# A fp32 diffusion block on one core: accumulators, weight rings, the cut of the feed-forward and the place of modulation units

## The chip, the core and the metric

The kernel runs on one core of one Trainium2 chip. The metric is the device time of one execution in microseconds (us). The five engines that matter here are TensorE (PE in the profile; PEld is its loading of weights), VectorE (DVE), ScalarE (ACT), GpSimd (POOL) and SyncE (SP), which issues nearly all DMAs, in the order of the program.

## What is computed

Two layers of a diffusion backbone over 512 main tokens and 256 context tokens, model width 1024. Each layer has a modulated norm, three token mixers (windowed attention, a bidirectional gated recurrence, a chunked MLP) merged by gates, an output projection, and a SwiGLU feed-forward of 2816 hidden columns. In the last layer only the main tokens are needed. The parts that the change touches are:

```python
g = sigmoid(gate)                                    # gate = h @ w_in[:, gate columns]
m = g0 * (a @ w_br[0]) + g1 * (b @ w_br[1]) + g2 * (c @ w_br[2])
x = x + g1mod * (m @ w_o)
h = rmsnorm(x, norm2_g[l]) * (1.0 + sc2) + sh2
x = x + g2mod * ((silu(h @ w_gate) * (h @ w_up)) @ w_down)
# sh1, sc1, g1, sh2, sc2, g2 = split(silu(c) @ w_ada[l] + b_ada[l], 6), and the same for the context
```

Everything is fp32.

## The kernel before

**Tiles.** Activations lie with channels on the partitions and tokens (T = 768, main and context together, in layer 1 512) along the free axis. A matrix product goes tile by tile: `dense` takes 128 output columns, loads their weights (`load_raw`, a DMA on SP's queue, L279), and computes over 8 (or 4, or 2) blocks of 128 input channels. fp32 is made of three matmuls of a short format: weights and activations are split into a high part (ACT, L288 and L349 for weights, L730 for activations) and a low part (VectorE, L289, L350, L731), and PE sums high x high, high x low and low x high (L306). A whole tile of 768 tokens needs columns of 512 and 256 in two PSUM banks, so a dense tile with 8 input blocks has 24 steps of two matmuls each.

**Weight buffers.** Pools `wraw`, `whi`, `wlo` hold 3, 2 and 2 slots of 4 KB per partition. A slot is taken for every weight tile whatever its size, and also for every block of modulation weights (`wra`, L535).

**The feed-forward of layer 0.** Its 22 hidden tiles are worked in pieces (`FF_PIECES[0]`): per piece the gate and up tiles, then the 8 down tiles of that piece, added to the residual `X` by VectorE (L778). The first `FF_PLAIN` tiles are plain `dense` tiles (L1333, L1336). All other tiles are taken in pairs by a scheme of seven products in place of eight (`seven`): the input channels, the two output tiles and the tokens are halved, and seven products of 4 input blocks x 128 columns x 384 tokens (`product`, 12 matmuls, L405) are combined. They come in the order B11, B21, N2, N1, T3, B22, T4 and use four sets of weights: g1 (B11, B21), g2 (N2, N1), g3 (T3, B22), g4 (T4 alone). g2 and g3 are split from sums of raw weights that POOL makes (`s21`, `s34`, L426). There are two sevens per pair, gate and up. Results are evacuated between the products: ACT copies partial results u1, u2 and u5 out of PSUM (L434, L440, L442), and `take` combines them on VectorE (L463, L465).

`al` and `ga`, the accumulators of B11+N2+T3+T4 and of N1+B22, are the two banks of one 1024-wide PSUM tile `pa`; `be` (B21) is a bank `pb` of its own. Waits are set by tile: an instruction that writes a tile waits until earlier readers of that tile have finished.

**Activation sums.** `seven_acts` makes the four sums N1, N2, T3 and T4 of the activations (POOL L370, VectorE L374 to L378) and splits them. It is a generator; before, its whole body for all four block pairs is issued behind the first plain tile.

**Modulation units.** The next layer's modulation vectors come from `ada_units`: a unit (512 columns of `w_ada`) is four steps; a step loads 512 KB (L536) and adds two blocks of it, scaled by one entry of silu(c), into an accumulator per token kind (`nb`) (the first block on ACT, L520, the others on VectorE, L522). The fourth step folds the accumulators (L497, L498), and the last unit of a group spreads the result (a matmul, L507). Steps wait in `ada_queue`, and `fill(n)` issues n of them at that place in the program. Layer 1's units 0 to 3 (nb 2, 16 steps) are queued behind layer 0's merge and issued at every down tile of layer 0's feed-forward. Units 4 to 7 and 8 to 11 (nb 1, 16 steps each) are queued at layer 1's merge (L1272) and issued two per merge tile (L1296).

**Order.** Each engine works its instructions in the order in which the program lists them; a scheduler puts them in that order from the code, and PE follows the code closely.

## Time and profile before

| | us |
|---|---|
| median of 3 runs | 2583.61 (2577.85 to 2583.71) |
| the profiled execution | 2584.96 |
| its span in the profile | 2583.0 |
| granted PE clock over the span | 0.987 |
| layer 0's feed-forward, first plain tile to the end | 905 to 1558 |
| layer 1's merge, about | 1960 to 2110 |

A row of waits reads: engine, what it was to write and in which line, what it waited for, then the sum of us, how often, and the longest. A row of the timeline reads: start, duration, engine, line, operation, output<-inputs, shape, and in brackets the idle time before and its releaser. A row of a group ends with count, busy us, mean ns, and idle time before.

### The profile page before, as it was taken

What the parts mean: (1) busy time and instruction counts of PE and PEld (TensorE: products, weight loads), DVE (VectorE), ACT (ScalarE), POOL (GpSimd) and SP (SyncE); (2) the same over time, 40 slices, a digit from 0 to 9 for tenths busy, and PEclk for the clock granted to TensorE, in tenths of its full rate; (3) what the DMA queues carried; (4) which work ended last, traced back from release to release, by engine and by line L of the source; (5) the groups of instructions that cost most, each with busy time, mean ns of one, the idle gap of its engine ahead of it and who ended that gap; (6) DMA issues with size and microseconds to landing.
All of it is one profiled execution on the core that took longest, in us unless ns stands there. A gap on an engine that the chain in (4) does not pass through costs nothing. (4 is left out here: it accounts for less than half of the span.)

```text
span 2583.0 us, 34315 instructions
## 1 busy us (share of the span) xinstructions
PE 2428.9 (94%) x13582; PEld 2088.2 (81%) x13582; DVE 1549.7 (60%) x2648; ACT 904.4 (35%) x1520; POOL 325.6 (13%) x231
## 2 busy tenths in 40 slices
PE   8899999999999978788989888999999899999998
PEld 4888888888888867777878777888787689888888
DVE  4688787764453576474444456767887655534335
ACT  3333354442222432323232234334544234322224
POOL 0001100000211240302112132010000112000001
PEclk9999999999999989999999999999999999999999
DMA  7222111123432313231212222111226644333234
GB/s 280 76 81 74 41 42 38 33 86 115 142 107 68 100 57 103 65 118 50 71 44 66 66 80 84 42 41 50 58 58 179 204 139 140 104 107 97 85 105 130
DMA packets 358031, 234.23 MB, mean 91 GB/s; under 512 B 8368, under 2 KB 329328, under 8 KB 357872
## 3 DMA queue, kind: packets, MB, share of 16 engines
q1 hardware_dynamic: 353936, 219.47, 28.6%
q0 software_dynamic: 2304, 10.49, 1.1%
q8 instruction: 107, 1.75, 0.3%
q10 hardware_dynamic: 1632, 2.10, 0.2%
q14 instruction: 52, 0.43, 0.1%
HBM read 224.68 MB, written 7.34 MB: 90 GB/s over the span
## 5 line engine op out<-in xcount | busy, mean ns | idle before, releaser
L288 ACT ACTIVATE wh<-wr 128x1024 fp32r<-128x1024 f32 (+4 forms) x340 | 301.7, 888 | 850.3 <-PE pd L306 604.1
L289 DVE TENSOR_TENSOR wl<-wr,wh 128x1024 fp32r<-128x1024 f32 (+4 forms) x340 | 350.7, 1033 | 209.0 <-ACT wh L288 205.7
L306 PE MATMUL pd<-hh,wh 128*128 128x512 f32 (+1 forms) x1504 | 461.8, 363 | 11.5 <-ACT gt L1282 7.2
L306 PE MATMUL pd<-hh,wl 128*128 128x512 f32 (+1 forms) x1504 | 451.1, 356 | 0.4
L306 PE MATMUL pd<-hl,wh 128*128 128x512 f32 (+1 forms) x1504 | 450.0, 355 | 0.0
L306 PEld LDWEIGHTS pd<-hh,wh 128*128 128x128 f32 x1504 | 249.0, 190 | 45.4 <-ACT gt L1282 10.1
L306 PEld LDWEIGHTS pd<-hh,wl 128*128 128x128 f32 x1504 | 249.6, 190 | 43.7 <-DVE wl L289 4.4
L306 PEld LDWEIGHTS pd<-hl,wh 128*128 128x128 f32 x1504 | 249.1, 190 | 34.2
L522 DVE SCALAR_TENSOR_TENSOR acc<-wra,sc,acc 128x512 f32<-128x512 f32 x224 | 166.3, 772 | 93.8 <-DMA wra<-in_w_ada 69.9
L306 PE MATMUL pd<-guh,wh 128*128 128x512 f32 (+1 forms) x576 | 172.8, 345 | 7.5 <-ACT wh L288 6.9
L306 PE MATMUL pd<-guh,wl 128*128 128x512 f32 (+1 forms) x576 | 171.4, 343 | 4.7 <-DVE wl L289 4.6
L306 PE MATMUL pd<-gul,wh 128*128 128x512 f32 (+1 forms) x576 | 170.7, 341 | 0.3 <-DVE gul L731 0.3
L306 PE MATMUL pd<-fl,wh 128*128 128x512 f32 (+1 forms) x432 | 160.7, 379 | 5.7 <-DVE fl L701 5.7
L306 PE MATMUL pd<-fh,wl 128*128 128x512 f32 (+1 forms) x432 | 160.2, 378 | 5.9 <-DVE wl L289 5.8
L306 PE MATMUL pd<-fh,wh 128*128 128x512 f32 (+1 forms) x432 | 159.3, 377 | 2.8 <-DVE silu L1337 2.2
L778 DVE SCALAR_TENSOR_TENSOR X<-pd,mod,X 128x256 f32<-128x256 f32 (+1 forms) x160 | 84.0, 559 | 111.5 <-PE pd L306 111.3
L306 PEld LDWEIGHTS pd<-guh,wh 128*128 128x128 f32 x576 | 98.1, 190 | 23.9 <-ACT wh L288 10.3
L306 PEld LDWEIGHTS pd<-guh,wl 128*128 128x128 f32 x576 | 98.3, 191 | 19.7 <-DVE wl L289 7.3
L306 PEld LDWEIGHTS pd<-gul,wh 128*128 128x128 f32 x576 | 98.1, 190 | 13.7 <-DVE gul L731 1.1
L405 PE MATMUL pa<-fh,wh 128*128 128x384 f32 x240 | 85.5, 356 | 24.9 <-DVE ptmp L463 7.3
L1294 POOL TENSOR_TENSOR macc<-macc,gt 128x768 f32<-128x768 f32 (+1 forms) x32 | 60.3, 1884 | 337.7 <-DVE gt L1291 331.1
L650 POOL TENSOR_TENSOR sqa<-sqa,sq 128x256 f32<-128x256 f32 (+1 forms) x40 | 50.8, 1269 | 412.5 <-ACT sq L648 412.4
(277 smaller groups left out, 4630.6 us busy)
## 6 DMA issues: line engine op xcount, KB each, us to landing
wr<-in_w_in SPq DMA_DIRECT2D x116, 512.0 KB, 3.8
wra<-in_w_ada SPq DMA_DIRECT2D x80, 512.0 KB, 3.8
wr<-in_w_ffn_gate SPq DMA_DIRECT2D x44, 512.0 KB, 3.9
wr<-in_w_ffn_up SPq DMA_DIRECT2D x44, 512.0 KB, 3.9
wr<-in_w_out SPq DMA_DIRECT2D x32, 512.0 KB, 3.7
wr<-in_w_branch SPq DMA_DIRECT2D x48, 256.0 KB, 3.1
wr<-in_w_ffn_down SPq DMA_DIRECT2D x40, 256.0 KB, 2.7
wr<-in_w_ffn_down SPq DMA_DIRECT2D x24, 384.0 KB, 3.1
```

What stands on the lines that cost most here:

```text
L288: nc.scalar.activation(out=h, in_=r, func=AF.Copy)
L289: nc.vector.tensor_tensor(out=o, in0=r, in1=h.bitcast(F32), op=ALU.subtract)
L306: nc.tensor.matmul(ps[:, b0:b1], lhsT=w[:, k, :], rhs=x[:, b0:b1], start=b not in first, stop=(k == kt - 1 and i == 2), skip_group_check=True)
L405: nc.tensor.matmul(out, lhsT=a[:, k0 + k, :], rhs=x, start=first, stop=(k == KD // 2 - 1 and i == 2), skip_group_check=True)
L522: nc.vector.scalar_tensor_tensor(out=acc[:, 0:512], in0=w, scalar=sc, in1=acc[:, 0:512], op0=ALU.mult, op1=ALU.add)
L650: eng.tensor_tensor(out=acc[:, c0:c1], in0=acc[:, c0:c1], in1=sq[:, c0:c1], op=ALU.add)
L778: self.nc.vector.scalar_tensor_tensor(out=self.X[m][:, c0:c1], in0=ps[:, c0:c1], scalar=gcol(b, m), in1=self.X[m][:, c0:c1], op0=ALU.mult, ...
L1294: nc.gpsimd.tensor_tensor(out=mm, in0=mm, in1=gt[:, 0:tt], op=ALU.add)
```

## The change

1. `ga` becomes a bank `pg` of its own, `al` the first half of a tile of its own. `ptmp` becomes one page of 768 in place of two: u5 takes the place of u1.
2. The three weight pools become rings of 12, 8 and 8 KB from which a tile takes only its own size (2 KB for 4 input blocks, 1 KB for 2).
3. `FF_PLAIN` goes from 2 to 4 and the pieces of layer 0 from (4,4,4,4,4,2) to (4,2,4,4,4,4): the first piece is four plain tiles, and 18 sevens are left of 20. `seven_acts` is issued a block pair at a time beside the second to fourth plain tile.
4. Modulation units 4 to 7 of layer 1 are queued with units 0 to 3 behind layer 0's merge. In layer 0's feed-forward a step is issued per pair of tiles by sevens and at every second down tile; in layer 1's merge one per tile, and none in the first branch.

```diff
--- before.py
+++ after.py
@@ -27,8 +27,8 @@
 HD = 64
 DK = 128
 LEVELS = 7
-FF_PIECES = ((4, 4, 4, 4, 4, 2), (5, 5, 6, 6))
-FF_PLAIN = 2
+FF_PIECES = ((4, 2, 4, 4, 4, 4), (5, 5, 6, 6))
+FF_PLAIN = 4
 H = T // 2
 NPAGES = 27
 BLOCK_US = 0.8
@@ -109,9 +109,9 @@
         self.cp = ctx.enter_context(tc.tile_pool(name="const", bufs=1))
         self.pages = Pages(ctx.enter_context(tc.tile_pool(name="pages", bufs=1)), NPAGES)
         self.dr = ctx.enter_context(tc.tile_pool(name="spill", bufs=1, space=bass.MemoryType.DRAM))
-        self.wr = ctx.enter_context(tc.tile_pool(name="wraw", bufs=3))
-        self.wh = ctx.enter_context(tc.tile_pool(name="whi", bufs=2))
-        self.wl = ctx.enter_context(tc.tile_pool(name="wlo", bufs=2))
+        self.wr = ctx.enter_context(tc.tile_pool(name="wraw", bufs=1)).ring(3 * D * 4, name="wrawr")
+        self.wh = ctx.enter_context(tc.tile_pool(name="whi", bufs=1)).ring(2 * D * 4, name="whir")
+        self.wl = ctx.enter_context(tc.tile_pool(name="wlo", bufs=1)).ring(2 * D * 4, name="wlor")
         self.sm = ctx.enter_context(tc.tile_pool(name="small", bufs=4))
         self.sp = ctx.enter_context(tc.tile_pool(name="parts", bufs=1))
         self.pd = ctx.enter_context(tc.tile_pool(name="psd", bufs=2, space=bass.MemoryType.PSUM))
@@ -275,16 +275,16 @@
 
 
     def load_raw(self, wap, kt):
-        raw = self.wr.tile([P, KD, P], F32, tag="wr", name=self.nm("wr"))
-        self.nc.sync.dma_start(out=raw[:, 0:kt, :], in_=wap.rearrange("(k p) c -> p k c", p=P))
+        raw = self.wr.tile([P, kt, P], F32, name=self.nm("wr"))
+        self.nc.sync.dma_start(out=raw, in_=wap.rearrange("(k p) c -> p k c", p=P))
         return raw
...
@@ -338,17 +338,12 @@
             self.step_chain()
 
 
-    def high_low(self, parts):
-
...
+    def high_low(self, src):
+
+        n = src.shape[1]
+        hi = self.wh.tile([P, n // P, P], F32R, name=self.nm("wh"))
+        lo = self.wl.tile([P, n // P, P], F32R, name=self.nm("wl"))
+        self.split(src, *(t.rearrange("p k c -> p (k c)") for t in (hi, lo)))
         return hi, lo
 
     def seven_acts(self, act):
@@ -359,35 +354,42 @@
...
+        held, last, whole = [], [], []
+        for k in range(KD // 2 + 1):
+            if k < KD // 2:
+                whole.append([self.single("b1"), self.single("b2")])
+                for r, (h, l) in zip(whole[k], (act[k], act[k + KD // 2])):
+                    nc.gpsimd.tensor_tensor(out=r[:, 0:T], in0=h[:, 0:T].bitcast(F32), in1=l[:, 0:T].bitcast(F32),
+                                            op=ALU.add)
+            if k > 0:
...
+            yield None
         for k, (t, t4) in enumerate(last):
             h1, l1 = act[k]
             self.split(t4, h1[:, H:T], l1[:, H:T])
@@ -424,29 +426,28 @@
         for o, x, y in ((s1, r2[:, 0:n], r2[:, n:2 * n]), (s2, s1, r1[:, 0:n]), (s3, r1[:, 0:n], r2[:, 0:n]),
                         (s4, s2, r1[:, n:2 * n])):
             nc.gpsimd.tensor_tensor(out=o, in0=x, in1=y, op=ALU.add)
-        ps = self.pd.tile([P, 1024], F32, tag="pd", name=self.nm("pa"))
-        al, ga = ps[:, 0:H], ps[:, 512:512 + H]
-        be = self.bank("pb")[:, 0:H]
-        tmp = self.pair("ptmp")
-        u1, u2, u5 = tmp[:, 0, 0:H], tmp[:, 0, H:T], tmp[:, 1, 0:H]
-        g1 = self.high_low([r1])
+        al = self.pd.tile([P, 1024], F32, tag="pd", name=self.nm("pa"))[:, 0:H]
+        be, ga = self.bank("pb")[:, 0:H], self.bank("pg")[:, 0:H]
+        tmp = self.single("ptmp")
+        u1, u2, u5 = tmp[:, 0:H], tmp[:, H:T], tmp[:, 0:H]
+        g1 = self.high_low(r1)
         self.product(al, g1, 0, q["B11"], True)
         nc.scalar.copy(out=u1, in_=al)
         self.product(be, g1, KD // 2, q["B21"], True)
         take(0, 0, be, u1)
-        g2 = self.high_low([s21])
+        g2 = self.high_low(s21)
         self.free(sa)
         self.product(al, g2, 0, q["N2"], False)
         nc.scalar.copy(out=u2, in_=al)
         self.product(ga, g2, KD // 2, q["N1"], True)
         nc.scalar.copy(out=u5, in_=ga)
-        g3 = self.high_low([s34])
+        g3 = self.high_low(s34)
         self.free(sb)
         self.product(al, g3, 0, q["T3"], False)
         take(1, 1, al, u5)
         self.product(ga, g3, KD // 2, q["B22"], False)
         take(0, 1, ga, u2)
-        g4 = self.high_low([r2[:, n:2 * n]])
+        g4 = self.high_low(r2[:, n:2 * n])
         self.product(al, g4, 0, q["T4"], False)
         take(1, 0, al, None)
         self.free(tmp)
@@ -488,6 +489,7 @@
                 self.split(s[:, t, 0:T], hp[:, t, 0:T], lp[:, t, 0:T])
                 gu.append((hp[:, t, :], lp[:, t, :]))
             self.free(s)
+            self.fill(1)
 
 
     def ada_fold(self, acc, part):
@@ -532,7 +534,7 @@
                 self.parts = self.sp.tile([P, 128], F32, tag="parts", name=self.nm("parts"))
             if q == 0:
                 state["accs"] = [self.single("acc") for _ in range(nb)]
-            raw = self.wr.tile([P, 2, 512], F32, tag="wr", name=self.nm("wra"))
+            raw = self.wr.tile([P, 2, 512], F32, name=self.nm("wra"))
             self.nc.sync.dma_start(out=raw, in_=self.a["w_ada"][l][q * 256:(q + 1) * 256, u * 512:(u + 1) * 512]
                                    .rearrange("(k p) c -> p k c", p=P))
             for k in (0, 1):
@@ -1269,7 +1271,7 @@
 
         macc = []
         if l == 1:
-            self.ada_queue += self.ada_units(1, (4, 5, 6, 7), 1) + self.ada_units(1, (8, 9, 10, 11), 1)
+            self.ada_queue += self.ada_units(1, (8, 9, 10, 11), 1)
         for bi, (idx, src) in enumerate(((2, cc), (0, at), (1, o))):
             if bi == 2:
                 self.x_back(tt)
@@ -1293,12 +1295,13 @@
                     mm = macc[m // 2][:, m % 2, 0:tt]
                     nc.gpsimd.tensor_tensor(out=mm, in0=mm, in1=gt[:, 0:tt], op=ALU.add)
                 self.free(gt)
-                self.fill(1 + l)
+                if l == 0 or bi > 0:
+                    self.fill(1)
             self.free(*brheld)
         self.free(*hheld)
         self.drain()
         if l == 0:
-            self.ada_queue += self.ada_units(1, (0, 1, 2, 3), 2)
+            self.ada_queue += self.ada_units(1, (0, 1, 2, 3), 2) + self.ada_units(1, (4, 5, 6, 7), 1)
         self.dump(f"m{l}", macc[0][:, 0, :])
         mact, mheld = self.split_pairs(macc, tt, "m")
         g1 = self.small("g1", 16).rearrange("p (b k) -> p b k", b=2)
@@ -1322,7 +1325,7 @@
         f0 = 0
         pieces = FF_PIECES[l]
         plain = FF_PLAIN if l == 0 else 2 * D_FF
-        quarters = qheld = None
+        making = self.seven_acts(act2)
         for pi, n in enumerate(pieces):
             last = pi == len(pieces) - 1
             gu, guheld = [], []
@@ -1341,12 +1344,14 @@
                 self.split(s[:, 0:tt], hp[:, i % 2, 0:tt], lp[:, i % 2, 0:tt])
                 self.free(s)
                 gu.append((hp[:, i % 2, :], lp[:, i % 2, :]))
-                if l == 0 and i == 0:
-                    making = self.seven_acts(act2)
+                if l == 1:
+                    self.fill(1)
+                elif i > 0:
                     next(making)
-                self.fill(0 if l == 0 else 1)
-            if l == 0:
-                if quarters is None:
+                    if i > 1:
+                        next(making)
+            if l == 0 and f0 + n > plain:
+                if f0 <= plain:
                     quarters, qheld = next(making)
                 self.seven_gate_up(l, range(max(f0, plain), f0 + n, 2), quarters, gu, guheld)
             if last:
@@ -1361,7 +1366,8 @@
                     ps = self.dense(a["w_ffn_down"][l][f0 * P:(f0 + n) * P, m * P:(m + 1) * P], gu, [blk[1:]])
                     for bb in ([blk] if last else blocks):
                         self.add_res(m, ps, lambda b, m: self.mod[l][:, 40 + m, b:b + 1], bb)
-                    self.fill(1)
+                    if l == 1 or m % 2:
+                        self.fill(1)
                 if last and bi == 0:
                     self.drain()
                 self.finish_chains()
```

PE's order at the boundary from product N2 to product N1, in the first seven of the program (`nh` and `nl` are high and low parts of the activation sums, `wh` and `wl` of the weights; `pa` holds `al` and `ga`). Before:

```order
L405 MATMUL pa_1402_8531<-nh_1385_8390,wh_1407_8565 128x384
L405 MATMUL pa_1402_8531<-nl_1386_8391,wh_1407_8565 128x384
L405 MATMUL pa_1402_8531<-nh_1385_8390,wl_1408_8566 128x384
L405 MATMUL pa_1402_8531<-nh_1364_8339,wh_1407_8565 128x384 [waits Activation_49]
L405 MATMUL pa_1402_8531<-nl_1365_8340,wh_1407_8565 128x384
L405 MATMUL pa_1402_8531<-nh_1364_8339,wl_1408_8566 128x384
L405 MATMUL pa_1402_8531<-nh_1371_8356,wh_1407_8565 128x384
```

Of the change, at the same place (`np` holds both parts of N1 and N2, `pg` is `ga`'s own bank):

```order
L407 MATMUL pa_1457_9057<-np_1406_8724,wl_1464_9093 128x384
L407 MATMUL pa_1457_9057<-np_1410_8736,wh_1463_9092 128x384 x2
L407 MATMUL pa_1457_9057<-np_1410_8736,wl_1464_9093 128x384
L407 MATMUL pg_1459_9059<-np_1386_8578,wh_1463_9092 128x384 x2
L407 MATMUL pg_1459_9059<-np_1386_8578,wl_1464_9093 128x384
L407 MATMUL pg_1459_9059<-np_1392_8594,wh_1463_9092 128x384 x2
L407 MATMUL pg_1459_9059<-np_1392_8594,wl_1464_9093 128x384
```

The first matmul of N1 has lost its wait for ACT; the matmuls are otherwise the same.

SP's order of DMAs over a piece with two pairs by sevens, from its first gate block (raw weights r1, r2 of gate, then of up, twice) to the first down weights. Before:

```order
L279 DMA wr_1480_9103<-in_w_ffn_gate 128x8x128 [waits DMAHW3_49,DVE_49]
L279 DMA wr_1481_9105<-in_w_ffn_gate 128x8x128 [waits DMAHW4_49,DVE_49]
L279 DMA wr_1495_9226<-in_w_ffn_up 128x8x128 [waits DMAHW5_49,DVE_49]
L279 DMA wr_1496_9228<-in_w_ffn_up 128x8x128 [waits DMAHW6_49,DVE_49,Pool_49]
L279 DMA wr_1513_9356<-in_w_ffn_gate 128x8x128 [waits DMAHW7_49,DVE_49]
L279 DMA wr_1514_9358<-in_w_ffn_gate 128x8x128 [waits DMAHW0_49,DVE_49,Pool_49]
L279 DMA wr_1528_9479<-in_w_ffn_up 128x8x128 [waits DMAHW1_49,DVE_49]
L279 DMA wr_1529_9481<-in_w_ffn_up 128x8x128 [waits DMAHW2_49,DVE_49,Pool_49]
L279 DMA wr_1545_9608<-in_w_ffn_down 128x4x128 [waits DMAHW3_49,DVE_49]
L536 DMA wra_1551_9643<-in_w_ada 128x2x512 [waits DMAHW4_49,DVE_49,Pool_49]
```

Of the change:

```order
L279 DMA wr_1531_9510<-in_w_ffn_gate 128x8x128 [waits DMAHW6_49,DMAHW5_49,DMAHW7_49,DVE_49,Activation_49]
L279 DMA wr_1532_9512<-in_w_ffn_gate 128x8x128 [waits DMAHW1_49,DMAHW0_49,DVE_49]
L279 DMA wr_1547_9634<-in_w_ffn_up 128x8x128 [waits DMAHW2_49,DVE_49]
L279 DMA wr_1548_9636<-in_w_ffn_up 128x8x128 [waits DMAHW3_49,DVE_49,Pool_49]
L538 DMA wra_1565_9764<-in_w_ada 128x2x512 [waits DMAHW4_49,DVE_49]
L279 DMA wr_1567_9771<-in_w_ffn_gate 128x8x128 [waits DMAHW5_49,DVE_49,Pool_49]
L279 DMA wr_1583_9895<-in_w_ffn_up 128x8x128 [waits DMAHW7_49,DVE_49]
L279 DMA wr_1568_9773<-in_w_ffn_gate 128x8x128 [waits DMAHW6_49,DVE_49]
L279 DMA wr_1584_9897<-in_w_ffn_up 128x8x128 [waits DMAHW0_49,DVE_49,Pool_49]
L538 DMA wra_1601_10025<-in_w_ada 128x2x512 [waits DMAHW2_49,DVE_49]
L279 DMA wr_1602_10031<-in_w_ffn_down 128x4x128 [waits DMAHW1_49,DVE_49,Pool_49]
```

A modulation load (`wra`) now stands behind each pair's up weights in that piece, ahead of the second pair's gate and ahead of the down weights, and the second pair's gate blocks no longer stand together: the first block of up stands between them.

VectorE's order where a gate seven ends and the up seven begins (the two `silu` rows at the top are the takes after the gate's T3 and B22, `wl` the low parts of up's g1 and g2, `acc` the parts of one modulation step, `ptmp<-pb` the first take of up). Before:

```order
L463 SCALAR_TENSOR_TENSOR silu_1479_9102<-pa_1484_9113,ptmp_1486_9115 128x384 [waits PE_49,Activation_49]
L465 TENSOR_TENSOR silu_1479_9102<-pa_1484_9113,ptmp_1486_9115 128x384 [waits PE_49]
L350 TENSOR_TENSOR wl_1503_9240<-wr_1495_9226,wh_1502_9239 128x1024 [waits DMAHW0_49,DVE_49,Activation_49]
L350 TENSOR_TENSOR wl_1505_9271<-s21_1497_9230,wh_1504_9270 128x1024 [waits DVE_49,PE_49,Activation_49]
L465 TENSOR_TENSOR ptmp_1501_9238<-pb_1500_9237,ptmp_1501_9238 128x384 [waits PE_49,Activation_49]
L481 TENSOR_TENSOR silu_1479_9102<-ptmp_1501_9238,silu_1479_9102 128x384 [waits DVE_49]
```

Of the change:

```order
L464 SCALAR_TENSOR_TENSOR silu_1530_9509<-pa_1535_9520,ptmp_1538_9523 128x384 [waits PE_49,Activation_49]
L466 TENSOR_TENSOR silu_1530_9509<-pg_1537_9522,ptmp_1538_9523 128x384 [waits PE_49]
L524 SCALAR_TENSOR_TENSOR acc_1527_9501<-wra_1565_9764,sc_136,acc_1527_9501 128x512 [waits DMAHW7_49]
L733 TENSOR_TENSOR wl_1556_9649<-wr_1547_9634,wh_1555_9648 128x1024 [waits DMAHW5_49,DVE_49,Activation_49]
L524 SCALAR_TENSOR_TENSOR acc_1528_9502<-wra_1565_9764,sc_136,acc_1528_9502 128x512
L733 TENSOR_TENSOR wl_1558_9680<-s21_1549_9638,wh_1557_9679 128x1024 [waits DVE_49,PE_49,Activation_49]
L524 SCALAR_TENSOR_TENSOR acc_1527_9501<-wra_1565_9764,sc_136,acc_1527_9501 128x512 [waits DVE_49]
L524 SCALAR_TENSOR_TENSOR acc_1528_9502<-wra_1565_9764,sc_136,acc_1528_9502 128x512 [waits DVE_49]
L466 TENSOR_TENSOR ptmp_1554_9647<-pb_1552_9645,ptmp_1554_9647 128x384 [waits PE_49,Activation_49]
```

Four `acc` instructions of one modulation step now stand between the gate's takes and the first take of up, the first of them ahead of the low part of up's first weights.

More of the change, by code (lines that the diff above doesn't have):

```diff
@@ L284, in load_w @@
         raw = self.load_raw(wap, kt)
-        hi = self.wh.tile([P, KD, P], F32R, tag="wh", name=self.nm("wh"))
-        lo = self.wl.tile([P, KD, P], F32R, tag="wl", name=self.nm("wl"))
-        r, h, o = (t.rearrange("p k c -> p (k c)")[:, 0:kt * P] for t in (raw, hi, lo))
+        hi = self.wh.tile([P, kt, P], F32R, name=self.nm("wh"))
+        lo = self.wl.tile([P, kt, P], F32R, name=self.nm("wl"))
+        r, h, o = (t.rearrange("p k c -> p (k c)") for t in (raw, hi, lo))
         nc.scalar.activation(out=h, in_=r, func=AF.Copy)
@@ L390, in seven_acts @@
-        yield None
+        held, last, whole = [], [], []
[6 more added lines that the diff above has]
+            if k > 0:
+                (h1, l1), (h2, l2) = act[k - 1], act[k + KD // 2 - 1]
+                q["B11"].append((h1[:, 0:H], l1[:, 0:H]))
+                q["B21"].append((h2[:, 0:H], l2[:, 0:H]))
+                q["B22"].append((h2[:, H:T], l2[:, H:T]))
+                r1, r2 = whole[k - 1]
+                n, t = self.single("n12"), self.single("t34")
+                n1, n2, t3, t4 = n[:, 0:H], n[:, H:T], t[:, 0:H], t[:, H:T]
+                nc.vector.tensor_tensor(out=n1, in0=r1[:, 0:H], in1=r1[:, H:T], op=ALU.subtract)
+                nc.vector.scalar_tensor_tensor(out=n2, in0=r2[:, H:T], scalar=-1.0, in1=n1, op0=ALU.mult,
+                                               op1=ALU.subtract)
+                nc.vector.tensor_tensor(out=t3, in0=r2[:, H:T], in1=r1[:, H:T], op=ALU.subtract)
+                nc.vector.scalar_tensor_tensor(out=t4, in0=n2, scalar=-1.0, in1=r2[:, 0:H], op0=ALU.mult,
+                                               op1=ALU.subtract)
+                self.free(r1, r2)
+                pair = self.pair("np", F32R)
+                held.append(pair)
+                if k % 2 == 1:
+                    tp = self.pair("tp", F32R)
+                    held.append(tp)
+                nh, nl, t3p = pair[:, 0, :], pair[:, 1, :], tp[:, 1 - k % 2, :]
+                self.split(n[:, 0:T], nh[:, 0:T], nl[:, 0:T])
+                self.split(t3, t3p[:, 0:H], t3p[:, H:T])
+                self.free(n)
+                q["N1"].append((nh[:, 0:H], nl[:, 0:H]))
+                q["N2"].append((nh[:, H:T], nl[:, H:T]))
+                q["T3"].append((t3p[:, 0:H], t3p[:, H:T]))
+                last.append((t, t4))
+            yield None
```

37 lines of the change are left out of this document (removed).

## The prediction

> **What bounds the kernel now.** I read the page's first part, then PE's waits, the timeline of the first seven-product tiles, and a table of windows over the stages the change touches.
>
> ```profile
> PE 2428.9 (94%) x13582; PEld 2088.2 (81%) x13582; DVE 1549.7 (60%) x2648; ACT 904.4 (35%) x1520; POOL 325.6 (13%) x231
> ```
>
> PE is busy 94% of the span, so only two things are to be had: fewer matmuls, or less of the remaining idle time. PE's waits, longest sums first (us in total, times, longest):
>
> ```profile
> core 0 of [0], span 2583.0 us
> PE pa L405 <- ACT ptmp L442: 18.7, 20, 1.0
> PE pa L405 <- ACT ptmp L440: 14.8, 20, 1.4
> PE pd L306 <- DVE wl L289: 11.8, 11, 5.5
> PE pd L306 <- ACT wh L288: 9.2, 9, 3.0
> PE pa L405 <- DVE ptmp L463: 7.3, 10, 0.7
> PE pa L405 <- DVE silu L463: 7.2, 10, 0.7
> ```
>
> Four of the six rows are matmuls of the seven products (L405), and each occurs 20 times or twice 10 times: once per use of the scheme (20 of them, two per pair of feed-forward tiles). In each, PE waits for an engine to finish reading one half of the PSUM tile `pa` before it writes the other. The timeline gives the price of the whole:
>
> ```profile
> 960.11 0.51 PE L306 MATMUL pd<-fh,wh 128*128 128x512 f32 x2
> 960.45 0.51 PE L306 MATMUL pd<-fl,wh 128*128 128x512 f32 x2
> ...
> 963.23 0.34 PE L405 MATMUL pa<-fh,wh 128*128 128x384 f32 x1
> ...
> 965.31 0.33 PE L405 MATMUL pb<-fh,wh 128*128 128x384 f32 x1
> ...
> 1052.43 0.62 PE L405 MATMUL pa<-t3p,wh 128*128 128x384 f32 x2 [0.96 <-ACT ptmp L442]
> ...
> 1071.00 0.61 PE L405 MATMUL pa<-t3p,wh 128*128 128x384 f32 x2 [0.91 <-ACT ptmp L442]
> ...
> 1558.29 0.79 PE L306 MATMUL pd<-hh,wh 128*128 128x512 f32 x1 [1.93 <-DVE nt L691]
> ```
>
> The first product starts at 963.23 and the second at 965.31 without a wait: one product (12 matmuls) costs 2.08 us, seven of them 14.56. But T3 of one seven to T3 of the next is 1071.00 - 1052.43 = 18.57 us. So each seven waits 4.01 us, and 20 of them 80. The stretch that the change rebuilds ends at 1558.29, where layer 1 begins: 1558.29 - 963.23 = 595.1 us. A dense step (one k tile of one of the three split products, 512 and 256 columns) takes 960.45 - 960.11 = 0.34 (0.345 over many), so a dense tile of 24 steps is 8.3.
>
> The windows (us, then busy time and instructions of PE, PEld, DVE, ACT, POOL, granted clock, DMA share, GB/s):
>
> ```profile
> 905.00:963.00 58.00, 43.59 (x227) 35.89 (x227) 44.78 (x60) 20.18 (x32) 23.52 (x14) 0.88 0.21 60
> 998.00:1041.00 43.00, 38.02 (x211) 32.92 (x212) 39.16 (x62) 8.56 (x13) 4.57 (x3) 0.98 0.49 147
> 1052.43:1089.62 37.19, 31.40 (x168) 28.84 (x168) 15.90 (x20) 12.69 (x19) 5.74 (x6) 1.00 0.20 57
> 1236.00:1270.00 34.00, 34.00 (x198) 29.98 (x197) 16.25 (x27) 7.18 (x10) 2.64 (x2) 1.00 0.29 85
> 1525.00:1560.00 35.00, 27.17 (x125) 19.45 (x123) 28.85 (x48) 22.07 (x45) 17.31 (x17) 0.92 0.49 155
> 1960.00:2110.00 150.00, 139.02 (x586) 108.76 (x585) 97.00 (x141) 43.06 (x64) 16.71 (x13) 0.97 0.64 188
> ```
>
> They are: the two plain tiles at the start of the feed-forward; a down stage with modulation steps; two sevens; a down stage without such steps; the last down stage of layer 0; the merge of layer 1. A down stage without modulation steps leaves PE full (34.00 of 34.00); with them PE stands 5.0 us idle and VectorE is 91% busy. That comparison is the price list for moving the modulation units.
>
> **The change, part by part.**
>
> *Accumulators.* `ga` gets a bank of its own, so N1 no longer waits for the copy of `al`, T3 for that of `ga`, B22 for the take of `al`, T4 for that of `ga`. The waits that are left (N2 on the copy of u1, T3 on that of u2, and so on) are one product, 2.08 us, older. In the window of two sevens, VectorE is 15.90 and ACT 12.69 busy of 37.19; two sevens at full speed last 29.1, so both still fit. I take the whole 4.01 as gone from the 18 sevens that stay. What is late next is the weights: two buffers of high and low parts, so the next pair can only be written when the pair before last is read.
>
> ```profile
> 978.65 0.34 PE L405 MATMUL pa<-fh,wl 128*128 128x384 f32 x1
> 978.90 1.06 ACT L349 ACTIVATE wh<-wr 128x1024 fp32r<-128x1024 f32 x1 [1.78 <-PE pa L405]
> ...
> 979.99 1.23 DVE L350 TENSOR_TENSOR wl<-wr,wh 128x1024 fp32r<-128x1024 f32 x1 [0.40 <-ACT wh L349]
> ```
>
> The high part starts 0.25 after the last matmul of the product that freed its buffer (978.65), the low part ends 2.57 after it. The tightest place is T4, alone between g3 and the next g1: 2.08, and the first low part is wanted two matmuls (0.35) later. That is short by 0.1 to 0.4 per seven.
>
> *The cut of the tiles.* Two sevens (29.1 free) become four dense tiles (4 x 8.3 = 33.2). Matmul time of the stretch, before: 20 x 14.56 = 291.2 and 22 down tiles of 24 steps, 22 x 24 x 0.345 = 182.2, together 473.4; so its waits are 595.1 - 473.4 = 121.7, of which 80 stand in the sevens and 41 elsewhere. After: 33.2 + 18 x 14.56 = 262.1 + 182.2 = 477.5 and its waits.
>
> *Modulation steps.* Layer 0's feed-forward now has 32 steps instead of 16: one per seven pair, and one at every second down tile, four a piece instead of eight. They are no longer only beside PE-bound matmuls.
>
> ```profile
> DVE acc L522 <- DMA wra<-in_w_ada: 69.9, 32, 5.8
> ```
>
> This is VectorE waiting for a step's weights: 2.2 us a time. In the new order of VectorE such an `acc` stands ahead of the low part of the next seven's weights (gate to up). From the rows: g4's buffers come free when T3 starts, its split is through about 1.5 us later, the load takes 3.8 to 3.9 (next fence), so `acc` can run 5.4 us behind T3's start, ends 0.75 later, and the low part of 1.23 is done at 7.4, wanted at 6.24 + 0.35: 0.8 late; I take 1.1 with handovers, six times, and 0.1 to 0.4 at the other boundaries: 8. [...]
>
> ```profile
> wr<-in_w_ffn_gate SPq DMA_DIRECT2D x44, 512.0 KB, 3.9
> ...
> L426 POOL TENSOR_TENSOR s<-s,wr 128x512 f32<-128x512 f32 x38 | 51.3, 1349 | 1.6
> L426 POOL TENSOR_TENSOR s<-wr,wr 128x512 f32<-128x512 f32 x19 | 29.2, 1536 | 121.5 <-DMA wr<-in_w_ffn_gate 63.1 <-DVE gul L731 50.0 <-PE pd L306 7.2
> ```
>
> The second pair of a piece pays once more: on SP's queue a modulation load now takes one of three raw slots ahead of the gate's second weight block, which is therefore asked for only when T4 of the seven before begins. Load 3.9, two POOL sums 1.54 + 1.35, high part 1.06: 7.85, while N2 is reached after 3 x 2.08 = 6.24. So 1.6 late, four times, and some 1.6 in the first pair behind the short piece: 8.
>
> The short piece (two tiles) now comes second, with four steps of two accumulators each, beside a down stage of half the matmuls. Its VectorE work per step, from the down stage at 998 to 1041 (same forms):
>
> ```profile
> L522 DVE SCALAR_TENSOR_TENSOR acc<-wra,sc,acc 128x512 f32<-128x512 f32 x24 | 16.8, 746 | 2.9 <-DMA wra<-in_w_ada 2.9
> L778 DVE SCALAR_TENSOR_TENSOR X<-pd,mod,X 128x512 f32<-128x512 f32 x8 | 5.9, 742 | 0.0
> L289 DVE TENSOR_TENSOR wl<-wr,wh 128x512 fp32r<-128x512 f32 x8 | 5.5, 684 | 0.0
> L778 DVE SCALAR_TENSOR_TENSOR X<-pd,mod,X 128x256 f32<-128x256 f32 x8 | 3.8, 476 | 0.0
> ```
>
> 16 acc x 0.746 = 11.9, X 9.7, half the low parts 2.8, folds about 2.7: 27.1, against 8 tiles x 6 steps x 0.345 = 16.6 of PE: 9 to 10 us late. The four-tile pieces have four steps (half of the window's 24 acc), 8 us less of VectorE than in that window, so I count 3 for all of them, 3 for the last piece and 4.5 for folding and spreading two groups. The other waits of the stretch (starts of pieces, clock) keep about 5. Sum: 8 + 8 + 9 + 3 + 3 + 4.5 + 5 = 40.5, about the 41 of before with other causes.
>
> So the stretch goes from 595.1 to 477.5 + 40.5 = 518: **-77**. Bounds of the 40.5: 25 (loads land in time) and 75 (VectorE bound in every down stage, 5 us each as at 998 to 1041, and each of nine pair steps at the mean 2.2).
>
> *Activation sums* spread beside three dense tiles. Today 14.4 us of 58 are idle in the front window at a clock of 0.88; one wait there is the 5.5 (`wl` of L289 behind the sums on VectorE). The sums take less than 45 us of VectorE and now have 50 of PE beside them (3 x 16.6). I take **-7**, between 0 (the sums still stand ahead of a low part) and -12.
>
> *Layer-1 merge* loses 16 of 32 steps and the step in its first branch. PE is idle 11.0 of 150 there, at 0.97. I take **-11**, between -3 (the loads of the gates, not the steps, are late) and -15 (clock back to 1 as well).
>
> *Costed at nothing:* the single `ptmp` page (u5 waits for u1's reader, two products back), the 2 KB fourth weight pair, and rings in the branch and down loads, which only start loads earlier. If the rings bring loads too early they collide at 188 GB/s in the merge; that is in its upper end.
>
> **Sum.** 2585.0 (the profiled run, span 2583.0; the median is 2583.6, 1.4 lower) - 77 - 7 - 11 = 2490, or 2489 on the median's scale. Low end: 477.5 + 25 in the stretch is -92.6, -12, -15: 2464. High end: 477.5 + 75 is -42.6, 0, -3: 2538.
>
> **Rivals.**
> *VectorE binds (0.2).* The steps in the sevens and the folds fall on the path wherever VectorE is near full. Its price: the stretch's waits at 65 to 75 rather than 40, so 2515 to 2540. For it: the 91% above. Against it: half as many steps per down stage.
> *The waits only move (0.07).* Weight pairs, not PSUM, set the period: it stays 18.57. Then 18 x 18.57 + 33.2 = 367.5 replaces 371.4, and with -18 elsewhere the time is 2562. For it: every `wh` in a seven waits for a product, as at 978.90. Against it: g1 and g2 have two products of time (4.16) for 2.57, and the 0.25 + 1.06 of the high part fits even T4.
> *Modulation loads on the path (0.03), slower.* Each of the 32 steps puts VectorE behind a load; if PE has to wait the whole 3.8 us of it, 32 x 3.8 = 122 goes on top of 2490: 2611. It ends faster than before as long as a step costs under 95 / 32 = 3.0 us. For it: single waits of 5.8 in the row above. Against it: eight steps in the down stage of 998 to 1041 left PE only 5.0 us idle.
>
> **How the numbers follow.** My own sum has 0.7 and a range of 2464 to 2515. The range for 8 in 10 takes in VectorE's rival up to 2530, and 2455 below for the sum's lower terms falling together. A change is told from none beyond about 0.3%, 7.8 us. The first two cases and the second rival (2562 is 0.8% less) are faster: 0.96; same 0.01, slower 0.03.
>
> **What would show it.** The rows of L407 (the new matmul line) waiting for ACT or VectorE should shrink from some 48 us (the four rows above) to under 10, and T3 to T3 be 14.6 to 15.5. VectorE's `acc` waits should grow inside the sevens. The short piece's down stage should be 27 to 30 us long with VectorE full. The merge of layer 1 should show PE over 97%. A period near 18.6 would make the first step wrong; a stretch longer than 553 us (477.5 + 75) the third.

## The result and the profile after

The changed kernel takes 2498.7 us (median of 4 runs, 2495.7 to 2504.4) beside 2582.4 of the kernel before: ratio 0.968, 95% interval 0.966 to 0.970. The profiled execution took 2495.7 us, its span is 2493.9. The first lines of its page:

```profile
span 2493.9 us, 34222 instructions
...
PE 2400.1 (96%) x13606; PEld 2084.2 (84%) x13606; DVE 1548.0 (62%) x2636; ACT 896.0 (36%) x1508; POOL 321.4 (13%) x223
```

and PE's longest waits:

```profile
PE pd L306 <- DVE wl L289: 15.3, 14, 2.5
PE pa L407 <- ACT ptmp L435: 7.9, 5, 2.6
PE tp L933 <- ACT vf L808: 7.3, 5, 2.6
PE pa L407 <- DVE wl L733: 7.1, 10, 1.6
```

All four rows by which the sevens waited for the readers of `pa` have gone from the list. What stands in their place is weights (`wl`, the low parts) and, five times, the copy of u1 ahead of N2.

The span divides into stages at the first matmul of each kind; the table reads those starts off the timelines (us):

| stage | before | after | change | forecast |
|---|---|---|---|---|
| up to layer 0's merge | 531.4 | 532.1 | +0.7 | 0 |
| merge, layer 0 | 303.0 | 308.1 | +5.1 | 0 |
| output projection, layer 0 | 74.5 | 72.9 | -1.6 | 0 |
| feed-forward, layer 0 | 646.7 | 562.6 | -84.1 | -84 |
| layer 1 up to its merge | 372.1 | 370.9 | -1.2 | 0 |
| merge, layer 1 | 229.1 | 215.1 | -14.0 | -11 |
| output projection, layer 1 | 49.4 | 49.5 | +0.1 | 0 |
| feed-forward, layer 1 | 376.8 | 382.5 | +5.7 | 0 |

One profile was taken of each kernel, and the same code differs between profiles. Layer 0's merge takes 299.2 to 303.1 us in the six profiles without a ring for raw weights and 307.2 to 312.5 in the eight with one; so a difference under some 4 us in one stage says little by itself.

Inside layer 0's feed-forward, sevens and down stages alternate. Each matmul is counted to the stage of its product, also where PE takes the first steps of a down tile ahead of the last product of a seven (us):

| | before | after | forecast for after |
|---|---|---|---|
| plain tiles at the front | 54.3 (two) | 76.9 (four) | 80.5 |
| sevens | 386.1 (20) | 288.4 (18) | 278 |
| down stages | 206.3 | 197.3 | 207 |

T3 to T3 of neighbouring sevens (13 or 14 such distances in a profile, those across a down stage left out) is 18.83 on average before and 16.24 after; a seven at full speed is 14.6.

### The profile page after: what moved, and what is told of

The parts are those of the page before. It is cut to its first block, busy times and chain, and to the rows that moved or that the text cites. A ratio compares the mean times of both kernels' runs of the same rounds, so it can differ in the third digit from the quotient of the medians.

```text
span 2493.9 us, 34222 instructions
## 1 busy us (share of the span) xinstructions
PE 2400.1 (96%) x13606; PEld 2084.2 (84%) x13606; DVE 1548.0 (62%) x2636; ACT 896.0 (36%) x1508; POOL 321.4 (13%) x223
## 5 line engine op out<-in xcount | busy, mean ns | idle before, releaser
L306 PE MATMUL pd<-hh,wl 128*128 128x512 f32 (+1 forms) x1504 | 448.3, 354 | 10.5 <-DVE wl L289 10.3
L306 PE MATMUL pd<-fl,wh 128*128 128x512 f32 (+1 forms) x496 | 176.8, 373 | 4.5 <-DVE fl L703 4.5
L306 PE MATMUL pd<-fh,wh 128*128 128x512 f32 (+1 forms) x496 | 175.7, 372 | 4.0 <-ACT wh L288 3.4
L306 PE MATMUL pd<-fh,wl 128*128 128x512 f32 (+1 forms) x496 | 175.5, 371 | 0.3 <-DVE wl L289 0.3
L306 PEld LDWEIGHTS pd<-guh,wl 128*128 128x128 f32 x576 | 99.4, 191 | 15.8 <-DVE wl L289 3.2
L306 PEld LDWEIGHTS pd<-fh,wh 128*128 128x128 f32 x496 | 89.9, 189 | 22.8 <-ACT wh L288 6.0
L306 PEld LDWEIGHTS pd<-fl,wh 128*128 128x128 f32 x496 | 90.4, 189 | 21.4 <-DVE fl L703 5.8
```

Source lines behind the costliest of these rows:

```text
L306: nc.tensor.matmul(ps[:, b0:b1], lhsT=w[:, k, :], rhs=x[:, b0:b1], start=b not in first, stop=(k == kt - 1 and i == 2), skip_group_check=True)
```

## Experiments

Every kernel was timed beside the kernel before; ratios are to it. "ff0" is layer 0's feed-forward, stages as in the table.

**1. The bank alone, in the kernel before.**

```diff
-        ps = self.pd.tile([P, 1024], F32, tag="pd", name=self.nm("pa"))
-        al, ga = ps[:, 0:H], ps[:, 512:512 + H]
-        be = self.bank("pb")[:, 0:H]
+        al = self.pd.tile([P, 1024], F32, tag="pd", name=self.nm("pa"))[:, 0:H]
+        be, ga = self.bank("pb")[:, 0:H], self.bank("pg")[:, 0:H]
```

> The kernel before with one edit: the accumulator ga in a PSUM bank of its own. Theory (the sevens' waits were for the readers of the other half of the shared tile): 20 sevens lose 4.0 us each, T3 to T3 falls from 18.6 to 14.6-15.2, the time falls by 70 to 80 us to 2503-2513, and PE's waits on L440, L442, L463 and L465 (58 us in all) nearly vanish. Rival (weight pairs set the period, the waits only move): the period stays above 17.5 and the time is 2560 or more.

2506.4 us, ratio 0.971 (0.970 to 0.972). ff0 is 572.9, so 73.8 shorter; nothing else moved by more than 2. Two sevens in the timeline of this kernel:

```profile
1335.52 0.51 PE L405 MATMUL pa<-t3p,wh 128*128 128x384 f32 x2
...
1350.21 0.51 PE L405 MATMUL pa<-t3p,wh 128*128 128x384 f32 x2
```

14.69 us, and neither T3 has a wait in brackets. The mean of 14 distances is 14.77. The first step of the prediction holds, and the rival by which the waits only move is out.

**2. The shared tile again, in the changed kernel** (the edit of 1 reversed).

> The changed kernel with al and ga again two banks of one PSUM tile. Theory: 18 sevens get back 4.0 us each, so 72 us more than the changed kernel: about 2570, and the other parts of the change are worth together 12 us or so against the kernel before. Rival (the new cut and the moved units carry a good part of the gain): 2530 or less.

2550.1 us, ratio 0.988 (0.987 to 0.990). ff0 went from 562.6 to 613.7: +51, not +72, between theory and rival. The longest of PE's waits over this kernel's sevens and down stages:

```profile
PE pa L407 <- ACT ptmp L444: 16.8, 18, 1.0
PE pa L407 <- ACT ptmp L442: 9.7, 17, 0.6
PE pa L407 <- DVE silu L465: 6.5, 9, 0.7
```

The waits on the shared tile are back (the first is 0.93 us each, as before), and T3 to T3 is 19.07, near the 18.83 of before. The difference lies in the changed kernel: its sevens take 16.24, not 14.7. 18 x (19.07 - 16.24) = 51. So of some 1.6 us per seven of other waits only 0.2 show when the tile is shared (19.07 - 18.83); the rest was hidden behind PSUM's waits, and with the tile divided it shows. Experiment 8 names these waits.

**3. Fixed slots in place of rings, in the changed kernel.**

```diff
-        self.wr = ctx.enter_context(tc.tile_pool(name="wraw", bufs=1)).ring(3 * D * 4, name="wrawr")
-        self.wh = ctx.enter_context(tc.tile_pool(name="whi", bufs=1)).ring(2 * D * 4, name="whir")
-        self.wl = ctx.enter_context(tc.tile_pool(name="wlo", bufs=1)).ring(2 * D * 4, name="wlor")
+        self.wr = ctx.enter_context(tc.tile_pool(name="wraw", bufs=3))
+        self.wh = ctx.enter_context(tc.tile_pool(name="whi", bufs=2))
+        self.wl = ctx.enter_context(tc.tile_pool(name="wlo", bufs=2))
...
```

(The lines that are left out give every weight tile a whole slot again.)

> The changed kernel with the weight pools as fixed slots of 4 KB (3, 2, 2) in place of the rings. Theory (the rings make a 4 KB tile wait where tiles of another size lie in the way): layer 0's merge falls from 308.1 to 303 us, layer 1's feed-forward from 382.5 to 377, so at least 10 us less than the changed kernel: 2488 or less. Rival (the deeper loads of the rings carry the down stages and the merge of layer 1, 14.0 us shorter in the changed kernel): these two stages still fall, but layer 0's feed-forward (562.7) and layer 1's merge (215.1) grow by 10 or more, and the time stays within 5 us of the changed kernel's 2499 or is above it.

2486.2 us, ratio 0.963 (0.961 to 0.965), faster than the changed kernel with intervals apart. The windows of merge and feed-forward (layer 0's merge, then layer 1's feed-forward; us, busy time of PE, PEld, DVE, ACT, POOL, clock, DMA share, GB/s), of the changed kernel:

```profile
532.10:840.20 308.10, 303.01 (x1731) 263.40 (x1730) 149.89 (x224) 79.34 (x111) 35.13 (x19) 0.99 0.35 103
...
2111.40:2493.90 382.50, 371.02 (x1824) 311.93 (x1822) 158.89 (x234) 115.49 (x169) 12.86 (x13) 0.99 0.35 101
```

and with fixed slots:

```profile
531.80:834.80 303.00, 302.93 (x1732) 263.00 (x1731) 148.94 (x224) 79.63 (x111) 35.08 (x19) 1.00 0.36 107
2108.60:2485.40 376.80, 368.66 (x1823) 312.51 (x1822) 159.12 (x234) 116.32 (x169) 12.60 (x13) 1.00 0.35 103
```

Both stages are back at the values of before; the same matmuls, 5.1 and 5.7 us apart. ff0 is 560.6 (2.0 less), layer 1's merge 220.3 (5.2 more). Inside ff0 the small difference hides two large ones: with fixed slots T3 to T3 is 15.22 and the sevens take 275.6 in place of 288.4, but the down stages take 207.3 in place of 197.3. So the rings help layer 1's merge and the down stages, and cost the sevens about what the down stages gain.

**4. Rings alone, in the kernel before** (the reverse of 3, and tiles of their own size as in the change).

> The kernel before with one edit: weight pools as rings of 12, 8 and 8 KB with tiles of their own size. Theory (rings cost where sizes alternate): layer 0's merge 303.0 to 308, layer 1's feed-forward 376.8 to 382, and layer 1's merge (229.1) gains at most 5, so 5 to 11 us slower than before. Rival (rings are what shortened layer 1's merge): layer 1's merge falls to 220 or less and the time is the same as before or less.

2592.0 us, ratio 1.004 (1.002 to 1.005): slower, by 0.4%. The time is in the theory's range, but not by its stages alone. Layer 0's merge 308.1, layer 1's feed-forward 382.4, and layer 1's merge 236.7, 7.6 more rather than a gain. But ff0 fell to 627.4, by 19.3, with T3 to T3 unchanged at 18.82: in most pieces of this kernel PE works 1.7 us of the first down tile ahead of the last T4 (0.3 before), and the last down stage is 22.8 instead of 30.7 us. The spans of the two profiled executions are only 2.0 us apart, the medians 10.5, so these stages don't account for the whole difference of the medians.

**5. The old cut**: `FF_PLAIN = 2`, pieces (4,4,4,4,4,2), all activation sums behind the first plain tile.

```diff
-FF_PIECES = ((4, 2, 4, 4, 4, 4), (5, 5, 6, 6))
-FF_PLAIN = 4
+FF_PIECES = ((4, 4, 4, 4, 4, 2), (5, 5, 6, 6))
+FF_PLAIN = 2
...
-                elif i > 0:
+                elif i == 0:
+                    for _ in range(5):
                         next(making)
-                    if i > 1:
-                        next(making)
```

> The changed kernel with two plain tiles, pieces (4,4,4,4,4,2) and all activation sums behind the first plain tile, as before. Theory (sums beside three dense tiles are worth 7 us, the cut itself costs 4 in matmuls and the short piece in second place some 9): layer 0's feed-forward 562.7 goes to 558-572 and the time is 2494 to 2510, so the new cut and the spread sums together are worth little. Rival (they carry the 10 us that layer 0's feed-forward gained beyond the own bank, 572.9 to 562.6): 2510 or more.

2500.9 us, ratio 0.970 (0.967 to 0.972), as the changed kernel. ff0 is 557.4, 5.2 less and just under the range. The time is as the theory has it, and the rival is out.

**6. Four plain tiles, but all sums behind the first** (the second half of that edit).

> The changed kernel, four plain tiles kept, with all activation sums behind the first plain tile. Theory (VectorE's sums stand ahead of the low part of the next dense tile): PE waits 5 to 8 us for wl in the second plain tile, and the time rises by 5 to 10 us over the changed kernel's 2499. Rival (four tiles hide the sums wherever they are issued): within 3 us of it.

2506.9 us, ratio 0.972 (0.970 to 0.974). ff0 568.7, 6.1 more than the changed kernel, with the wait that was foreseen, a little under its range, in this kernel's timeline:

```profile
950.89 1.01 PE L306 MATMUL pd<-fh,wl 128*128 128x512 f32 x2 [4.91 <-DVE wl L289]
```

So spreading the sums is worth 6 us of ff0 with four plain tiles (8 in the medians). And since ff0 of 5 (old cut, sums at once) stands 11.3 below that of 6, the new cut as such costs about 11 in ff0 with rings; the medians put it at 6.

**7. Units 4 to 7 back at layer 1's merge.**

```diff
-            self.ada_queue += self.ada_units(1, (8, 9, 10, 11), 1)
+            self.ada_queue += self.ada_units(1, (4, 5, 6, 7), 1) + self.ada_units(1, (8, 9, 10, 11), 1)
...
-                if l == 0 or bi > 0:
-                    self.fill(1)
+                self.fill(1 + l)
...
-            self.ada_queue += self.ada_units(1, (0, 1, 2, 3), 2) + self.ada_units(1, (4, 5, 6, 7), 1)
+            self.ada_queue += self.ada_units(1, (0, 1, 2, 3), 2)
```

> The changed kernel with units 4 to 7 again queued at layer 1's merge, two steps per tile there; layer 0's feed-forward keeps the new places of the steps but has only 16. Theory (steps cost on both sides): layer 1's merge grows from 215.1 by 9 to 15, layer 0's feed-forward falls from 562.7 by 8 to 12, the time stays within 5 us of 2499. Rival A (steps are hidden in the feed-forward): it doesn't fall, and the time rises by 10 or more. Rival B (the merge was shortened by the rings, not by the units): the merge stays below 220.

2512.9 us, ratio 0.975 (0.973 to 0.978). ff0 554.1 (8.5 less, as in the theory), layer 1's merge 237.8 (22.7 more, well over it). The merge is as long as in experiment 4, with rings and the old places.

**8. Steps at down tiles alone**: no step in the seven pairs, one at every down tile from the second piece on.

```diff
             self.free(s)
-            self.fill(1)
...
-                    if l == 1 or m % 2:
+                    if l == 1 or pi > 0 or m % 2:
```

> The changed kernel with no modulation step in the seven pairs and one at every down tile from the second piece on. Theory (a load in the pair delays N2 of the next gate, and an acc holds up the next low part, 16 us in all; a down stage with eight steps is VectorE-bound): PE's waits on the copy of u1 (7.9) and on wl of the sevens (7.1) fall below 5 together, the short piece's and the next two down stages lose 12, 5 and 5, so the time is 2495 to 2510. Rival (steps beside down tiles are cheaper than in the pairs): 2490 or less.

2498.3 us, ratio 0.969 (0.967 to 0.971), as the changed kernel. T3 to T3 falls to 14.68 on average, 1.56 less, which is 20 us over the 13 distances; all sevens together take 270.4 in place of 288.4. So the steps in the pairs cost some 18 us of the sevens, and ff0 is only 7.0 shorter: the down stages take 210.7 in place of 197.3. Layer 1's merge is 3.8 longer.

**9. Raw weights in the ring, high and low parts in fixed slots.**

```diff
-        self.wh = ctx.enter_context(tc.tile_pool(name="whi", bufs=1)).ring(2 * D * 4, name="whir")
-        self.wl = ctx.enter_context(tc.tile_pool(name="wlo", bufs=1)).ring(2 * D * 4, name="wlor")
+        self.wh = ctx.enter_context(tc.tile_pool(name="whi", bufs=2))
+        self.wl = ctx.enter_context(tc.tile_pool(name="wlo", bufs=2))
...
```

> The changed kernel with the raw weights still in a ring of 12 KB, but the high and low parts in two fixed slots of 4 KB each. Theory A (the rings of 8 KB for high and low parts make a 4 KB tile wait for two smaller ones; the raw ring only loads earlier): layer 0's merge 303 and layer 1's feed-forward 377 as with fixed slots, layer 1's merge at most 217, so 2480 to 2486. Theory B (the raw ring is at fault, loads start too late): layer 0's merge 307 or more, layer 1's feed-forward 381 or more, and 2492 or more.

2500.3 us, ratio 0.969 (0.967 to 0.971). Neither theory holds whole; each has a stage. In this kernel's windows:

```profile
535.20:843.40 308.20, 301.42 (x1731) 262.34 (x1730) 149.80 (x224) 79.35 (x111) 35.14 (x19) 1.00 0.35 103
2125.20:2502.00 376.80, 368.67 (x1824) 312.43 (x1822) 159.09 (x234) 116.31 (x169) 12.86 (x13) 1.00 0.35 103
```

The raw ring costs the 5 us of layer 0's merge (308.2), the rings for high and low parts the 5.7 of layer 1's feed-forward (back at 376.8). ff0 was 568.3, longer than with all rings (562.6) or none (560.6): its sevens take 16.22 from T3 to T3, as with all rings, and its down stages 201.7, between the two.

**10, 11. Fixed slots and steps at down tiles alone (the edits of 3 and 8); and the same with the old cut (5) and a step at every down tile of the first piece too.**

> Fixed slots, and the modulation steps beside down tiles alone (both edits apart were -12.6 and -0.4 in the medians; layer 0's feed-forward was 2.0 and 7.0 shorter). If the gains add up: layer 0's feed-forward about 554, layer 1's merge 220, 2479. Rival (with fixed slots the steps in the pairs cost less, so nothing is left to gain): layer 0's feed-forward 560 and 2486 or more.

> As the last, with the pieces, the plain tiles and the sums of before. If the old cut is worth the 5.2 us that it was with rings: layer 0's feed-forward 549 and 2474. Rival (the short piece at the end, with the norm behind it, or eight steps a piece cost what the matmuls save): 2479 or more.

2487.7 us, ratio 0.965 (0.964 to 0.966), and 2493.2, ratio 0.967 (0.965 to 0.969). T3 to T3 is at its floor (14.73 and 14.67), but ff0 is 564.8 and 570.8: with fixed slots the down stages and the first products behind them lose more than the steps had cost, and the old cut is no gain either. The rival holds in both.

**12. Fixed slots, units 4 to 7 back at the merge** (the edits of 3 and 7).

> Fixed slots, and units 4 to 7 back at layer 1's merge. With rings that edit cost 14 us (merge 22.7 longer, layer 0's feed-forward 8.5 shorter), but the rings alone had made the old merge 7.6 longer. Theory (the move itself is worth little; the rings made the old place dear): layer 1's merge goes from 220.3 to 229 as before the change, layer 0's feed-forward from 560.6 to 552, and the time is within 4 us of the 2486 of fixed slots. Rival (the move pays by itself): 2495 or more.

2486.0 us, ratio 0.964 (0.962 to 0.966), equal to experiment 3. ff0 552.4, the merge 224.4 where 229 was expected. Moving the units is worth nothing measurable once the rings are gone; it was worth 14 us only because the rings had made the old place dear. Experiments 3 and 12 are the fastest versions, 0.5% below the changed kernel.

## Why the prediction came out

2489 was forecast, 2498.7 measured, inside the range. The mechanism was right in the main term. Behind it the steps in the pairs fell on other places than forecast, the gain at layer 1's merge had another cause, and the rings, which were costed at nothing, cost more than the miss.

Of the signs that the prediction named, three failed: PE's L407 rows wait 15.0 us (7.9 + 7.1), not under 10; T3 to T3 is 16.24, above 15.5; and the short piece's down stage is shorter than 27 us. One held: PE is busy 209.66 of the 215.10 us of layer 1's merge, 97.5%. One price was wrong in itself: waits of 65 to 75 us in the stretch would have made the first rival's time 2514 to 2524, not 2515 to 2540.

**Accumulators: right.** Forecast 4.01 us per seven for 18 sevens, 72. Alone (1) the bank gave 73.8 for 20, 3.7 each. Inside the changed kernel it is worth 51 (2), since other waits show once PSUM's are gone. That the weights are next in line was right as well: `wl` L733 is one of the two waits that remain.

**Steps in the pairs: right in sum, wrong in place.** Forecast were 8 us mostly from gate to up, and 8 mostly at a second pair's gate. The nine distances of T3 from gate to up are only 5 us over 9 x 14.65. The worst place was named (N2 of a second pair's gate, after a late load), but priced at 1.6 where the distances of T3 are 19.07, 20.56, 17.36 and 17.38, together 15.8 over 4 x 14.65. The raw ring has a part in this that the prediction didn't see. With the raw weights alone in a ring (9) the same four distances are 17.53, 20.71, 17.38 and 17.37; with fixed slots (3) they are 14.63, 15.99, 14.80 and 14.61, though the steps stand in the same places. In the table, a row is a kernel (us):

| kernel | T3 to T3 | sevens | down stages |
|---|---|---|---|
| changed: rings, steps in the pairs | 16.24 | 288.4 | 197.3 |
| raw ring alone, steps in the pairs (9) | 16.22 | 288.7 | 201.7 |
| fixed slots, steps in the pairs (3) | 15.22 | 275.6 | 207.3 |
| rings, no steps in the pairs (8) | 14.68 | 270.4 | 210.7 |
| fixed slots, no steps in the pairs (10) | 14.73 | 277.5 | 212.8 |

With rings the steps cost the sevens 18 us, with fixed slots nothing that the sums show, so that 16 were forecast is luck. The loads on SP's queue at the first such place differ. Changed kernel, then fixed slots:

```profile
1099.32 0.37 SPq L279 DMA_DIRECT2D wr<-in_w_ffn_gate  x1
1102.41 0.37 SPq L279 DMA_DIRECT2D wr<-in_w_ffn_up  x1
1108.66 0.37 SPq L279 DMA_DIRECT2D wr<-in_w_ffn_gate  x1
...
1097.66 3.45 SPq L279 DMA_DIRECT2D wr<-in_w_ffn_gate  x2
1107.68 4.96 SPq L279 DMA_DIRECT2D wr<-in_w_ffn_up  x2
```

In the changed kernel up's first block goes ahead of the gate's second, which is asked for 1.41 us behind the start of T3 (1107.25) of the seven before; with fixed slots both gate blocks are asked for by 1101.11, 4.46 ahead of that T3 (1105.57). Without steps in the pairs (8) the rings too keep the gate's blocks together in every second pair, so it takes the ring and the step's load for this order; why the order comes out so stays open.

The changed kernel's timeline at the first place (the POOL rows are the sums of raw weights, L428; `wh` is the high part of g2):

```profile
1113.17 1.87 POOL L428 TENSOR_TENSOR s<-wr 128x512 f32<-128x512 f32 x1 [17.20 <-DMA wr<-in_w_ffn_gate]
...
1115.01 2.00 POOL L428 TENSOR_TENSOR s<-wr,wr 128x512 f32<-128x512 f32 x1
...
1116.97 2.62 POOL L428 TENSOR_TENSOR s<-s,wr 128x512 f32<-128x512 f32 x2
1118.28 1.06 ACT L732 ACTIVATE wh<-s 128x1024 fp32r<-128x1024 f32 x1 [4.63 <-POOL s L428]
1119.24 0.83 ACT L732 ACTIVATE guh<-silu 128x768 fp32r<-128x768 f32 x1
...
1119.98 0.46 ACT L435 COPY ptmp<-pa 128x384 f32<-128x384 f32 x1
...
1120.49 0.76 PE L407 MATMUL pa<-np,wh 128*128 128x384 f32 x2 [2.60 <-ACT ptmp L435]
```

Here three sums stand ahead of g2's high part (1.87, 2.00, 1.31), not two at 1.54 and 1.35; then on ACT's queue a split of the pair before and the copy of u1 come behind that high part, and N2 needs the copy. The sum of the prediction left out the third sum and the copy's place in the queue.

**Short piece: right.** Forecast 9 to 10 us over 16.6 of PE (its own terms, 27.1 - 16.6, give 10.5). Its down stage lasts 25.5 us, 8.9 over, with VectorE busy 22.68 of 25.47. PE is busy 21.71 for its 16.6 of matmuls; the granted clock of 0.87 is some 3 of this difference (an estimate, 0.13 x 21.71):

```profile
1055.41:1080.88 25.47, 21.71 (x97) 17.25 (x98) 22.68 (x40) 4.52 (x8) 0.23 (x1) 0.87 0.35 103
```

All down stages together were 10 us cheaper than forecast, which with 3.6 at the front covers the 10 us that the sevens cost more; the 3 that are left come mostly from where the stretch was taken to end (1558.29, in the table 1555.63). So the stage's -84 is right by offsetting errors, and that the sum agreed to 0.1 is luck.

**Sums beside plain tiles: right.** Forecast -7; the front needed 76.9 instead of the 54.3 + 33.2 = 87.5 of the same tiles at the old rate, -10.6, and experiment 6 puts the spread alone at 6 in ff0 (10.3 in the front).

**Layer-1 merge: right in size, wrong in cause.** Forecast -11 for half the steps; -14.0 measured. With fixed slots the merge goes from 229.1 to 220.3 (3), and only 4.1 of that is the units (12 against 3), which are paid back in layer 0's feed-forward (552.4 against 560.6, 8.2). The merge of 12 is 4.7 shorter than that of before with the same steps: 2.5 of this is PE's pace (217.7 us busy at a clock of 0.98 against 215.2 at 0.99), and why 2.2 less is idle stays open.

**Rings at nothing: wrong, and large enough for the whole miss.** The prediction said that rings "only start loads earlier". They cost 5.1 in layer 0's merge and 5.7 in layer 1's feed-forward, 10.8 together, where the median was missed by 9.7; with fixed slots (3) the time is 2486.2, 2.8 under the forecast. The second is plain in ACT's rows of layer 1's feed-forward where a down stage of 128x640 tiles ends and 128x1024 tiles begin. Changed kernel:

```profile
2196.98 2.00 ACT L288 ACTIVATE wh<-wr 128x1024 fp32r<-128x1024 f32 x2 [9.46 <-PE pd L306]
...
2198.09 0.50 PE L306 MATMUL pd<-fh,wh 128*128 128x512 f32 x1 [0.92 <-ACT wh L288]
```

with fixed slots:

```profile
2190.46 1.06 ACT L288 ACTIVATE wh<-wr 128x1024 fp32r<-128x1024 f32 x1 [2.66 <-PE pd L306]
2193.86 1.06 ACT L288 ACTIVATE wh<-wr 128x1024 fp32r<-128x1024 f32 x1 [2.34 <-PE pd L306]
```

In slots, each large tile takes the place of one smaller tile and is split one down tile apart. In the ring both large ones are split only when the last down tile is read, back to back, and PE waits. The same wait comes at all three changes from down tiles to the next piece, 3.4 us in all, and at none of them with fixed slots; the rest of the 5.7 is not accounted for. That a tile of 4 KB lies over two smaller ones in a ring of 8 fits this, but no trace shows the addresses. In layer 0's merge, where the raw ring alone does it (9), PE waits three times for a low part, 4.9 us of the 5.1, and not at all with fixed slots. The changed kernel's timeline shows the chain at the longest of the waits:

```profile
756.48 0.37 SPq L538 DMA_DIRECT2D wra<-in_w_ada  x1
...
760.37 2.08 DVE L524 SCALAR_TENSOR_TENSOR acc<-wra,sc,acc 128x512 f32<-128x512 f32 x3 [3.92 <-DMA wra<-in_w_ada]
...
762.36 1.22 DVE L289 TENSOR_TENSOR wl<-wr,wh 128x1024 fp32r<-128x1024 f32 x1
...
763.64 0.62 PE L306 MATMUL pd<-hh,wl 128*128 128x512 f32 x2 [2.52 <-DVE wl L289]
```

The modulation load is issued at 756.48, the three `acc` wait for it 3.92 us, and the low part whose high part was ready since 757.06 (756.00 + 1.06) stands behind them, so PE waits 2.52. It is the third rival's mechanism, small and in another stage. In the last 3.31 us of the wait for the load (757.06 to 760.37) the high part was there and VectorE stood idle: the low part did not go ahead of the waiting `acc`. Why the raw ring issues that load so late, by which block's release, stays open.

## What to carry to other kernels

Where waits are set by tile, two accumulators in one tile make the writer of one wait for the readers of the other (73.8 us over 20 sevens in experiment 1); divide them before counting instructions, and then look for the waits that were hidden behind the wait that goes (here some 1.3 us a seven). A ring of tiles of mixed sizes doesn't only load earlier: here large tiles came later at the three changes from down tiles to the next piece in layer 1 (3.4 us of PE's waits), and the order of the loads changed too, so price it at both. A step that only moves has to be measured at both places; here, with fixed slots, the gain at one was the loss at the other.
